# Blocks beyond the third of an expert: from every turn to the end of the stage

## The chip, the cores and the metric

The kernel runs on one core of a Trainium2 chip. TensorE (PE) multiplies matrices; PEld is its loading of weights. VectorE (DVE), ScalarE (ACT) and GpSimd (POOL) do the element-wise work, and SyncE (SP) issues most DMA transfers. Each engine runs its own list of instructions in order and waits for others at semaphores. The metric is the time of one execution on the device in microseconds (us).

## The reference

Two layers run over 512 tokens of width 1024 (256 latent, 256 context). Each layer mixes the tokens (convolutions, gating, attention) and then sends every token to two of 16 experts; the router is shared. The change concerns the experts of the first layer alone.

```python
def moe_ffn(h, w_router, router_bias, w_gate, w_up, w_down):
    """Sigmoid router with bias-corrected, group-limited selection: best group, then top-2 experts in it."""
    s = jax.nn.sigmoid((h @ w_router).astype(F32))
    sel = s + router_bias.astype(F32)
    grp = sel.reshape(*sel.shape[:-1], N_EXPERT_GROUPS, EXPERTS_PER_GROUP)
    grp_score = jnp.sum(lax.top_k(grp, GROUP_SCORE_TOPK)[0], axis=-1)
    best = jnp.argmax(grp_score, axis=-1)
    in_group = (jnp.arange(N_EXPERTS) // EXPERTS_PER_GROUP) == best[..., None]
    _, idx = lax.top_k(jnp.where(in_group, sel, -jnp.inf), TOP_K)
    w = jnp.take_along_axis(s, idx, axis=-1)
    w = w / jnp.sum(w, axis=-1, keepdims=True)
    gates = jnp.sum(jax.nn.one_hot(idx, N_EXPERTS, dtype=F32) * w[..., None], axis=-2).astype(h.dtype)
    y = jnp.zeros_like(h)
    for e in range(N_EXPERTS):
        a = jax.nn.silu(h @ w_gate[e]) * (h @ w_up[e])
        y = y + gates[..., e:e + 1] * (a @ w_down[e])
    return y
...
        hf = rms_norm(x_mid, norm2_g[l]) * (1.0 + sc2) + sh2
        x = x_mid + g2 * moe_ffn(hf, w_router, router_bias, exp_w_gate[l], exp_w_up[l], exp_w_down[l])

        if not last:
            spectra_ctx = hyena_filter_spectra(n_ctx, *filt)
            ctx_mid = ctx + cg1 * mix_tokens(proj_ctx, k_ctx, v_ctx, None, spectra_ctx, lp)
            hc = rms_norm(ctx_mid, norm2_g[l]) * (1.0 + csc2) + csh2
            ctx = ctx_mid + cg2 * moe_ffn(hc, w_router, router_bias, exp_w_gate[l], exp_w_up[l], exp_w_down[l])
```

## The kernel before

The expert stage of the first layer takes the experts one after the other, in the order of the table TURNS, each in one call of `turn_0` (L1671). An expert's tokens are done in blocks of 64 (BLK); P is 128. Since only the chip knows how many tokens an expert got, the counts `cnt` are computed there (L1373 and L1374) and each engine loads the count of the next turn into a register (`counted`, L1828) and branches on it:

- `tc.If(cv > BLK, label=f"turn{p}")` at L1736: with over 64 tokens the If is taken (two blocks), otherwise the Else (one block). The other side of the code is jumped over.
- inside the If, `tc.If(cv > P, ...)` at L1762 (L1754 in the last turn): a third block, with its own Else.
- inside that, `tc.If(cv > P + BLK)` at L1772 (L1757 in the last turn): `overflow` (L1612), a loop over all further blocks (L1640). Its code stands in each of the 16 turns.

`tc.mark_branch_hint_location` (L1729 for the turn's If, L1737 for the third block) puts a hint ahead of a branch, on PE, DVE and ACT. PE, DVE and ACT run in the order in which the code is written (`tc.manual_schedule`).

An expert's weights are six pieces of 1 MB, loaded on SP's queue by the class `Stream` (`main`). `done(n)` releases the n oldest pieces, and `pump` issues as many further loads as slots are free (L183), each waiting for the last use of its slot. Where the branch decides which code runs, `repeat` issues the same loads on the other sides (L202). So the loads of a turn follow its `main.done(4)` in SP's list: behind the third block where that is run, behind `main.repeat()` in each Else.

`mm_in` makes an expert's hidden values (its matmuls carry L1538), `mm_out` its outputs (L1562), `put` sends a block's outputs to memory (copy L1444, indirect DMA L1445), `turn` transposes gathered tokens (L1522). At the end of the last turn `parts` forms `st` from the last outputs (L1580, L1581) and `add` puts them to the token stream (matmuls L1591, adds L1596 and L1597), with `stat` on ScalarE (L1834). L574 makes a small table for the second layer. In the second layer the experts go through another function, with a branch at L1862 around its rarer blocks.

Of the kernel before, what the change touches and what calls it, by code (L numbers as in the profile page):

```python
# [22 lines left out]
NE = 16  # L23
# [100 lines left out]
def hybrid_block_kernel(ctx: ExitStack, tc: tile.TileContext, xin, const, fconst, par, fpar, misc, fng,  # L124
# [979 lines left out]
    def project(l, T, S, yh, yl, split, mm3, hx, hf, hp, spare):  # L1104
# [3 lines left out]
        with ExitStack() as pctx:  # L1108
# [261 lines left out]
            b2 = bank()  # L1370
            for t in range(T):
                nc.tensor.matmul(b2[:, :16], lhsT=ones, rhs=M[:, t], start=(t == 0), stop=(t == T - 1))
            cnt = rp.tile([P, 16], I32, name="cnt", tag="cnt")  # L1373
            V.tensor_copy(cnt, b2[:, :16])  # L1374
            if dump is not None:
                dump(f"sc{l}", sc.rearrange("p t e -> p (t e)"))
                dump(f"gw{l}", gw.rearrange("p t e -> p (t e)"))
# [12 lines left out]
    def moe(l, cnt, idx, gc, pd, pk, rk, hx, h0, hp):  # L1390
# [5 lines left out]
        with ExitStack() as mctx:  # L1396
# [274 lines left out]
            def turn_0(p, e, cv, w, b0):  # L1671
# [64 lines left out]
                with tc.If(cv > BLK, label=f"turn{p}") as branch:  # L1736
# [14 lines left out]
                    if last:  # L1751
                        parts(b1, more[0])
                        mm_out(w, AT[0], out)
                        with tc.If(cv > P, label=f"third{p}"):  # L1754
                            add(more, last=True)
                            block(e, w, turn(X, 0, BLK, h=h0), g3[:, e:e + 1], C("slot", 2, 3), *temp, last=True)
                            with tc.If(cv > P + BLK):  # L1757
                                overflow(e, w, cv, P + BLK, *temp, last=True)
                            zero(OT[1])
                        main.done(4)  # L1760
                    else:
                        with tc.If(cv > P, label=f"third{p}") as branch2:  # L1762
                            turn(X, 0, BLK, h=h0)
                            put(b1, rows[1][:, e:e + 1])
                            b3 = mm_in(w, h0, tag="tp")
                            act(b3, g3[:, e:e + 1], AM[1])
                            head(0)
                            spin(AM[1], AT[1])
                            head(1)
                            put(mm_out(w, AT[1], bank("ob")), rows3[:, e:e + 1])  # L1770
                            mm_out(w, AT[0], out)
                            with tc.If(cv > P + BLK):  # L1772
                                overflow(e, w, cv, P + BLK, *temp)
                            main.done(4)
                        with branch2.Else():
                            main.repeat()
                            put(b1, rows[1][:, e:e + 1])
                            head(0, 1)
                            mm_out(w, AT[0], out)
                with branch.Else():  # L1780
                    first({4: lambda: vector(0), 6: lambda: vector(1)})
                    main.repeat()
                    if last:
                        where(e, OT[0], C("slot", 0, 1))
                        where(e, OT[1], C("slot", 1, 2))
                    scaled()
                    if start:
                        spin(AM[0], AT[0])
                        mm_out(w, AT[0], out)
                        for q in (1, 2):  # L1790
                            prepare(q, 0)
                            prepare(q, 1)
                        head(0, 1)
                    else:
                        head(0)
                        prepare(p + 2, 0)
                        spin(AM[0], AT[0])
                        prepare(p + 2, 1)
                        head(1)
                        mm_out(w, AT[0], out)  # L1800
# [11 lines left out]
                if not last:  # L1812
                    main.done(2)
                    return ncv, nw, b2
                parts(out, ST[0])
                for t in range(T):
                    add(owed, more, only=[t], last=True)
                    if t:
# [317 lines left out]
```

## Time and profile before

| | us |
|---|---|
| median of three executions (1350.97 to 1355.32) | 1351.72 |
| the profiled execution: time | 1359.33 |
| the profiled execution: span | 1357.5 |
| PE busy in the span (85%) | 1156.3 |
| DVE busy | 537.9 |
| ACT busy | 314.8 |
| POOL busy | 294.3 |

The expert stage of the first layer lies between about 479 and 829 us of the span, the second layer behind it. The turns differ: turn 2 has a third block, turns 3, 10, 14 and 15 have two blocks, the other eleven have one. A view of waits names the instruction that stood still, what it was released by, and how long it stood; "issue" is waiting for nothing that the profile shows, and an engine's name with a q (PEq, DVEq, PEldq) is its queue of control instructions: branches (COMPARE_BRANCH), register loads (TENSOR_LOAD) and semaphores. Times of such instructions aren't in the busy times. The rows on which the prediction rests stand below.

### The profile page before, as it was taken

Reading aid. Unit: us, or ns where it says so; the run is one execution under the profiler, and the core shown is the slowest. Engines: PE = TensorE matmul, PEld = TensorE weight load, DVE = VectorE, ACT = ScalarE, POOL = GpSimd, SP = SyncE. Lnnn points to the kernel's source line nnn. Section 1 sums busy time; section 2 is a strip of 40 time slices with the busy share of each in tenths; the row PEclk is TensorE's granted clock in tenths of the full one; section 3 lists DMA queues with packets and bytes.
Section 4 is the critical chain, followed back from the end, with each engine's and each line's share of the span. In section 5 each row is a group of like instructions: output and inputs, shape, how many; then the busy total and the mean of one; then the engine's idle time right before and its main releaser. Section 6 shows DMA issues by size and latency. Waiting matters only on the chain. (4 is left out here: it accounts for less than half of the span.)

```text
span 1357.5 us, 16560 instructions
## 1 busy us (share of the span) xinstructions
PE 1156.3 (85%) x6205; PEld 646.1 (48%) x6205; DVE 537.9 (40%) x1068; ACT 314.8 (23%) x569; POOL 294.3 (22%) x238
## 2 busy tenths in 40 slices
PE   6799998888899788978898977878787799988985
PEld 2456565556688433323333424756675433332321
DVE  4430966335323521100011047685535244433444
ACT  2422233223212111001111115324423111111111
POOL 4332232322033121111112064434224000000000
PEclk9999998888799788988899996889868899998997
DMA  9574453312572786599999645211236399947961
GB/s 361 199 302 184 156 186 101 132 62 94 217 279 72 297 340 218 175 384 393 383 396 395 260 141 192 93 63 55 98 126 264 141 409 402 393 187 291 403 267 47
DMA packets 48574, 310.85 MB, mean 229 GB/s; under 512 B 6017, under 2 KB 6209, under 8 KB 14096
## 3 DMA queue, kind: packets, MB, share of 16 engines
q1 hardware_dynamic: 41936, 292.77, 55.7%
q0 software_dynamic: 6320, 15.27, 4.3%
q8 instruction: 105, 1.72, 0.5%
q10 hardware_dynamic: 144, 0.52, 0.1%
q14 instruction: 69, 0.57, 0.1%
HBM read 297.99 MB, written 12.32 MB: 229 GB/s over the span
## 5 line engine op out<-in xcount | busy, mean ns | idle before, releaser
L603 POOL TENSOR_TENSOR ws<-w,ws 128x1024 fp32r<-128x1024 f32 x50 | 121.4, 2440 | 218.0 <-ACT ws L602 200.7
L1538 PE MATMUL b_pj<-w,HE 128*64 128x512 f32 x416 | 109.7, 665 | 23.3 <-issue 23.3
L234 PE MATMUL b_pj<-hh,ws 128*128 128x512 f32 (+1 forms) x448 | 123.0, 364 | 1.1 <-POOL ws L603 1.1
L1562 PE MATMUL b_sc<-w,rows 128*64 128x512 f32 x448 | 106.2, 615 | 2.7 <-ACT rows L1552 2.7
L693 DVE SCALAR_TENSOR_TENSOR cacc<-gl,pr,cacc 128x512 f32<-128x512 f32 (+1 forms) x120 | 92.6, 772 | 2.6
L234 PEld LDWEIGHTS b_pj<-hh,ws 128*128 128x128 f32 x448 | 79.9, 199 | 21.0 <-issue 9.7
L234 PE MATMUL b_pj<-hl,ws 128*128 128x512 f32 (+1 forms) x224 | 78.8, 352 | 0.0
L1538 PEld LDWEIGHTS b_pj<-w,HE 128*64 128x64 f32 x416 | 34.5, 151 | 85.3 <-issue 83.9
L602 ACT ACTIVATE ws<-w 128x1024 fp32r<-128x1024 f32 x50 | 52.5, 1052 | 70.2 <-PE b_pj L234 44.6
L1600 DVE TENSOR_TENSOR x<-b_ob,x 128x512 f32<-128x512 f32 x68 | 44.0, 687 | 61.8 <-PE b_ob L1591 61.6
L277 POOL TENSOR_TENSOR rf<-rf,half 128x1 f32<-128x1 f32 x2 | 1.1, 552 | 309.1 <-DVE rf L276 309.1
L1538 PE MATMUL b_pj<-w,hf 128*64 128x512 f32 x224 | 56.6, 644 | 10.4 <-PEq L1862 7.6
L1562 PEld LDWEIGHTS b_sc<-w,rows 128*64 128x64 f32 x448 | 31.5, 141 | 62.0 <-issue 57.5
L1445 POOL DMA_INDIRECT sums<-y,rws x19 | 29.8, 1567 | 137.4 <-DVE y L1444 123.1
L1538 PE MATMUL b_pj<-w,x 128*64 128x512 f32 x224 | 55.6, 617 | 1.8 <-PEq L1862 1.0
L234 PE MATMUL b_md<-w,sT 128*32 128x256 f32 x704 | 54.2, 433 | 1.3 <-DVE mT L313 1.3
L1545 DVE SCALAR_TENSOR_TENSOR X<-X,gc,b_pj 64x512 f32<-64x512 f32 x16 | 12.1, 754 | 108.2 <-ACT X L1544 108.2
L1444 DVE COPY y<-b_sc 128x512 f32<-128x512 f32 x15 | 10.4, 692 | 102.9 <-PE b_sc L1562 62.3
L234 PEld LDWEIGHTS b_pj<-hl,ws 128*128 128x128 f32 x224 | 44.6, 199 | 5.3
L1591 PE MATMUL b_ob<-st,ohT 128*128 128x512 f32 x76 | 32.7, 496 | 16.3 <-DVE st L1581 9.3
L1544 ACT ACTIVATE X<-b_pj 64x512 f32<-64x512 f32 x16 | 9.4, 589 | 158.4 <-PE b_pj L1538 150.7
L1544 ACT ACTIVATE cst<-b_pj 64x512 f32<-64x512 f32 x17 | 10.1, 592 | 145.6 <-PE b_pj L1538 145.6
(471 smaller groups left out, 2070.4 us busy)
## 6 DMA issues: line engine op xcount, KB each, us to landing
w<-in_exps_dram SPq DMA_DIRECT2D x168, 1024.0 KB, 11.4
w<-in_ada_dram SPq DMA_DIRECT2D x48, 1024.0 KB, 4.8
w<-in_win_dram SPq DMA_DIRECT2D x16, 1024.0 KB, 5.1
hold<-in_exps_dram SPq DMA_DIRECT2D x12, 1024.0 KB, 15.8
w<-in_wout_dram SPq DMA_DIRECT2D x8, 1024.0 KB, 4.7
hf<-in_exps_dram SPq DMA_DIRECT2D x6, 1024.0 KB, 8.0
cst<-in_exps_dram SPq DMA_DIRECT2D x6, 1024.0 KB, 8.7
pr<-in_par_dram SPq DMA_DIRECT2D x2, 1461.5 KB, 8.9
```

Of the source, the lines that this page charges most:

```text
L234: nc.tensor.matmul(out_, lhsT=lhsT, rhs=rhs, **kw)
L602: nc.scalar.activation(wh[:, :n], src, AF.Copy)
L603: nc.gpsimd.tensor_tensor(wl[:, :n], src, wh[:, :n].bitcast(F32), op=OP.subtract)
L693: nc.vector.scalar_tensor_tensor(ac, gl[:, :, j:j + L], R("cvw", i * 31 + j, i * 31 + j + 1), ac, op0=OP.mult, op1=OP.add)
L1444: V.tensor_copy(y, b)
L1445: nc.gpsimd.indirect_dma_start(out=sums[:, :], out_offset=bass.IndirectOffsetOnAxis(ap=row, axis=0), in_=y, in_offset=None, bounds_check=1 ...
L1538: nc.tensor.matmul(b[64 * j:64 * j + 64], lhsT=x, rhs=w[k // 2][:, at:at + 512], start=(k == 0), stop=(k == 7), tile_position=(0, 64 * j))
L1544: nc.scalar.activation(a[64:], b[:64], AF.Silu)
L1545: V.scalar_tensor_tensor(a[64:], a[64:], gate[64:], b[64:], op0=OP.mult, op1=OP.mult)
L1562: nc.tensor.matmul(b[64 * j:64 * j + 64], lhsT=aT[:, f, :], rhs=w[4 + f // 2][:, at:at + 512], start=(f == 0), stop=(f == 3), tile_positio ...
L1591: nc.tensor.matmul(b, lhsT=ohT[:, t * P:(t + 1) * P], rhs=st[h], start=(i == 0), stop=(i == len(blocks) - 1))
L1600: V.tensor_tensor(y[:, cs], b, y[:, cs], op=OP.add)
```

## The change

The overflow test leaves the third block of every turn. The code runs once, after `parts` in the last turn, under one test of the largest count: `cnt` gets a 17th column with the maximum (a reduction and a copy on DVE, in both layers). Under that test there is, for each of the 16 experts, an If that loads the expert's six pieces of weights again and runs `overflow`. `main.done(4)` of the last turn moves behind it, out of the If of two blocks, and `main.repeat()` of the last turn's Else goes. Line numbers of the new kernel are three higher than the old from L1376 on, so that L1736 is its L1739, and L1581 its L1584; from the new test on they differ by more (the new test is at L1815, the 16 Ifs at L1820).

```diff
@@ -1370,8 +1370,11 @@
             b2 = bank()
             for t in range(T):
                 nc.tensor.matmul(b2[:, :16], lhsT=ones, rhs=M[:, t], start=(t == 0), stop=(t == T - 1))
-            cnt = rp.tile([P, 16], I32, name="cnt", tag="cnt")
-            V.tensor_copy(cnt, b2[:, :16])
+            cnt = rp.tile([P, 17], I32, name="cnt", tag="cnt")
+            V.tensor_copy(cnt[:, :16], b2[:, :16])
+            most = rt("most")
+            V.tensor_reduce(most[:, 0:1], b2[:, :16], axis=AX.X, op=OP.max)
+            V.tensor_copy(cnt[:, 16:17], most[:, 0:1])
             if dump is not None:
                 dump(f"sc{l}", sc.rearrange("p t e -> p (t e)"))
                 dump(f"gw{l}", gw.rearrange("p t e -> p (t e)"))
@@ -1754,10 +1757,7 @@
                         with tc.If(cv > P, label=f"third{p}"):
                             add(more, last=True)
                             block(e, w, turn(X, 0, BLK, h=h0), g3[:, e:e + 1], C("slot", 2, 3), *temp, last=True)
-                            with tc.If(cv > P + BLK):
-                                overflow(e, w, cv, P + BLK, *temp, last=True)
                             zero(OT[1])
-                        main.done(4)
                     else:
                         with tc.If(cv > P, label=f"third{p}") as branch2:
                             turn(X, 0, BLK, h=h0)
@@ -1769,8 +1769,6 @@
                             head(1)
                             put(mm_out(w, AT[1], bank("ob")), rows3[:, e:e + 1])
                             mm_out(w, AT[0], out)
-                            with tc.If(cv > P + BLK):
-                                overflow(e, w, cv, P + BLK, *temp)
                             main.done(4)
                         with branch2.Else():
                             main.repeat()
@@ -1779,7 +1777,8 @@
                             mm_out(w, AT[0], out)
                 with branch.Else():
                     first({4: lambda: vector(0), 6: lambda: vector(1)})
-                    main.repeat()
+                    if not last:
+                        main.repeat()
                     if last:
                         where(e, OT[0], C("slot", 0, 1))
                         where(e, OT[1], C("slot", 1, 2))
@@ -1813,6 +1812,17 @@
                     main.done(2)
                     return ncv, nw, b2
                 parts(out, ST[0])
+                with tc.If(nc.values_load(cnt[0:1, 16:17], engines=engs, min_val=0, max_val=N) > P + BLK):
+
+                    add(more, last=True)
+                    for q in range(NE):
+                        ce = counted(q)
+                        with tc.If(ce > P + BLK):
+                            for i in range(6):
+                                nc.sync.dma_start(w[i], source("exp", l, 6 * q + i))
+                            overflow(q, w, ce, P + BLK, *temp, last=True)
+                    zero(OT[1])
+                main.done(4)
                 for t in range(T):
                     add(owed, more, only=[t], last=True)
                     if t:
```

The list of SP in turn 2, before: the test at L1772 with the loop of `overflow` (L1640) stands between the branch of the third block and the loads of L183, and the two groups of L202 are those of the Else sides.

```order
L1736 COMPARE_AND_BRANCH
L1762 COMPARE_AND_BRANCH
L1772 COMPARE_AND_BRANCH
L1640 COMPARE_AND_BRANCH
L1640 UNCONDITIONAL_BRANCH x2
L2132 BRANCH_PREFETCH_HINT
L1640 REGISTER_ALU
L1640 COMPARE_AND_BRANCH
L1640 UNCONDITIONAL_BRANCH
L1772 UNCONDITIONAL_BRANCH
L183 DMA w<-in_exps_dram 128x2048 x2
L183 DMA hold<-in_exps_dram 128x2048 x2
```

What SP meets between the third block's branch and the next loads is, there, the test and its loop, each with waits for the other engines.

The same place after: the branch of the third block (now printed at L1762, as `branch2` starts three lines earlier) is followed by the loads.

```order
L183 DMA w<-in_exps_dram 128x2048
L1739 COMPARE_AND_BRANCH
L1762 COMPARE_AND_BRANCH
L183 DMA w<-in_exps_dram 128x2048 x2
L183 DMA hold<-in_exps_dram 128x2048 x2
L1762 UNCONDITIONAL_BRANCH
```

On SP, PE, DVE, ACT and POOL alike the test and the loop are gone from the place between the third block's last work and the release of the weights.

The list of DVE at the end of the last turn, before: the end of the If (L1736), the small table L574, `st` of L1581, and the first adds.

```order
L1718 TENSOR_TENSOR cst<-cst,G_3410 128x1024
L1736 UNCONDITIONAL_BRANCH
L574 SCALAR_TENSOR_TENSOR aT<-mT_69,msc 128x4 x4
L1581 TENSOR_TENSOR st_9314<-b_sc,st_9314 64x512
L1581 TENSOR_TENSOR st_9315<-b_sc,st_9315 64x512
L1596 TENSOR_TENSOR HE_3413<-b_ob,G_3410 128x512
```

After, the part ahead of the new test (HE, G and x are tiles; `st_7727` and `st_7728` are the halves of st):

```order
L1721 TENSOR_TENSOR cst<-cst,G_3413 128x1024
L1739 UNCONDITIONAL_BRANCH
L1584 TENSOR_TENSOR st_7727<-b_sc,st_7727 64x512
L1584 TENSOR_TENSOR st_7728<-b_sc,st_7728 64x512
L1815 TENSOR_LOAD cnt
L1815 COMPARE_AND_BRANCH
L1599 TENSOR_TENSOR HE_3416<-b_ob,G_3413 128x512
```

`st` has moved up, and the branch stands where L574 stood. The part behind the jump over the overflow block:

```order
L1820 UNCONDITIONAL_BRANCH
L1834 TENSOR_SCALAR ohT_3422<-cst 128x512
L1815 UNCONDITIONAL_BRANCH x2
L574 SCALAR_TENSOR_TENSOR aT<-mT_69,msc 128x4 x4
L1599 TENSOR_TENSOR HE_3416<-b_ob,G_3413 128x512
```

So `st` moves ahead of L574; the load of the largest count and the branch L1815 stand between them, and L574 stands between the branch and the first adds. The branch passes 571 rows of DVE's list. In the compiled program the jump of PE over the If of a turn passes 584 or 585 instructions before and 402 to 406 after in the turns that end in the Else (368 in turn 0), and the new jump at the end passes 3251.

## Rows read from the trace of the kernel before

**Rows 1.** Windows, core 0: stretch, its length, busy us (xcount) by engine, PEclk, DMA share, GB/s

```profile
540.00:560.00 20.00, 18.64 (x94) 6.50 (x92) 2.14 (x3) 2.17 (x4) 3.13 (x2) 1.00 0.14 17
...
580.00:620.00 40.00, 31.45 (x142) 11.52 (x140) 3.58 (x5) 4.34 (x8) 7.67 (x6) 0.91 1.03 381
620.00:660.00 40.00, 31.53 (x132) 11.28 (x130) 3.58 (x5) 4.33 (x8) 6.77 (x5) 0.89 1.02 394
```

**Rows 2.** Waits of PE from 484 to 800: who waited for whom, us, times, longest

```profile
PE b_pj L1538 <- issue: 25.8, 10, 5.8
...
PE b_pj L1538 <- DMA w<-in_exps_dram: 2.4, 1, 2.4
...
PE b_md L1538 <- DVE y L1444: 1.7, 1, 1.7
```

**Rows 3.** Branches of line L1736, all and from 485: count, ns min/median/max, first and last start

```profile
L1736 PEldq COMPARE_BRANCH  x16: 76/5946/7167, 488.4 to 782.0; - x16
...
L1736 PEldq COMPARE_BRANCH  x1: 3342/3342/3342, 488.4 to 488.4; - x1
```

**Rows 4.** Timeline of PE at 583 and 646: start, us, engine, line, operation [idle before]

```profile
582.32 2.74 PE L1562 MATMUL b_sc<-w,rows 128*64 128x512 f32 x12
590.89 1.97 PE L1538 MATMUL b_pj<-w,HE 128*64 128x512 f32 x4 [5.83 <-issue]
...
645.88 2.36 PE L1538 MATMUL b_pj<-w,HE 128*64 128x512 f32 x10 [0.91 <-issue]
```

**Rows 5.** Other branches of PE, lines L1772, L1762 and L1754, columns as in rows 3

```profile
L1772 PEldq COMPARE_BRANCH  x1: 243/243/243, 555.5 to 555.5; - x1
...
L1762 PEldq COMPARE_BRANCH  x8: 68/376/2271, 538.7 to 781.4; - x8
...
L1754 PEldq COMPARE_BRANCH  x2: 187/1816/3444, 804.3 to 808.9; - x2
```

**Rows 6.** Page, part 3: the instruction queue: packets, MB, share

```profile
q8 instruction: 105, 1.72, 0.5%
```

**Rows 7.** Waits of the DMA queue of SyncE from 470 to 830

```profile
SPq L183 <- PEq L1772: 35.6, 1, 35.6
```

**Rows 8.** Line L1538 from 484 to 800: the projections that use h, columns as in rows 3

```profile
L1538 PE MATMUL b_tp<-w,h x16: 592/592/643, 543.0 to 546.1; 128*64 128x512 f32 x16
...
L1538 PE MATMUL b_tp<-hold,h x16: 592/592/593, 546.5 to 549.5; 128*64 128x512 f32 x16
```

**Rows 9.** Timeline of VectorE (DVE) at 560

```profile
560.09 0.69 DVE L1444 COPY y<-b_sc 128x512 f32<-128x512 f32 x1 [2.83 <-PEq L1772]
```

**Rows 10.** Timelines of PE, DVE and GpSimd (POOL) at 805 to 817, and line L574

```profile
805.10 3.60 PE L1562 MATMUL b_sc<-hold,rows 128*64 128x512 f32 x16
815.50 0.80 PE L1591 MATMUL b_ob<-st,ohT 128*128 128x512 f32 x1 [6.80 <-DVE st L1581]
...
810.99 3.75 DVE L574 SCALAR_TENSOR_TENSOR aT<-mT,msc 128x4 f32<-128x4 f32 x4 [0.74 <-DVEq L1754]
...
816.11 0.69 DVE L1581 TENSOR_TENSOR st<-b_sc,st 64x512 fp32r<-64x512 f32 x1 [0.66 <-ACT st L1580]
816.83 0.69 DVE L1596 TENSOR_TENSOR HE<-b_ob,G 128x512 f32<-128x512 f32 x1
...
814.60 1.99 POOL L1719 TENSOR_TENSOR x<-x,cst 128x1024 f32<-128x1024 f32 x1
...
L574 DVE SCALAR_TENSOR_TENSOR aT<-mT,msc x4: 148/764/2301, 811.0 to 814.6; 128x4 f32<-128x4 f32 x4
```

**Rows 11.** DVE: the cast of the counts, and the loads of a count into a register

```profile
479.19 0.17 DVE L1374 CAST cnt<-b_tp 128x16 int32<-128x16 f32 x1 [1.59 <-PE b_tp L1372]
...
L1828 DVEq TENSOR_LOAD <-cnt x16: 300/306/582, 482.0 to 760.1; - x16
```

**Rows 12.** Branches of line L1862 (second layer), and who waited for them (us, times)

```profile
L1862 PEldq COMPARE_BRANCH  x16: 89/3386/6276, 1062.4 to 1340.7; - x16
...
  PE b_pj L1538: 17.6, 12
```

## Prediction

> **What bounds the kernel now.** I read the busy times by stage first. In the expert stage of the first layer TensorE (PE) works 31.45 and 31.53 us of two 40 us stretches while the DMA engines are full, and 18.64 of 20 where they are nearly idle [rows 1]. So something takes PE's time there, and the view of waits says what: the matmuls of L1538 stood still 25.8 us in ten places "on issue", that is on nothing but PE's own queue, and once 2.4 us on a weight load [rows 2]. The branch instruction of L1736 explains these: PE's 16 take from 76 ns to 7.17 us, median 5.95 [rows 3]. The cheap ones are in the five turns that go into the If (more than 64 tokens), the dear ones in the eleven that jump over it to the Else. The timeline shows one at its worst: matmuls end at 585.06, the next starts at 590.89, 5.83 us later, and nothing else was late [rows 4]. Usually the branch begins while matmuls of some 3.6 us are still queued, so that of 6 us about 2.4 are seen. Weights land in time all along; a faster load gives nothing by itself. VectorE, ScalarE and GpSimd matter at the two ends of the stage alone.
>
> **What the change takes out of the turns.** In the compiled program PE's jump over the If passes 584 instructions in the old kernel and about 404 in the new one, because some 180 instructions of overflow code leave every turn. What does a jump of 404 cost? The rows give both ends. A jump of 179 (L1772) took 0.24 us, those of L1762 (up to 354, announced long ahead by a hint) 0.38 us in the median [rows 5]. The jump of 584 takes 3.34 us with idle DMA engines and 6 to 7 with busy ones [rows 3]. Instructions arrive in packets of 16.4 KB (1.72 MB in 105) [rows 6], which is 256 instructions of 64 bytes. A jump of 584 (2.28 packets) always lands two or three packets on; one of 404 (1.58) lands in the very next packet when it starts in the first 42% of its own, and two on otherwise. A next packet comes in order anyhow during a turn of 15 us, so I count such a jump as one of the cheap rows, and the others as they are now. The ten turns with a gap lose 25.8 + 2.4 - 0.9 (one wait of 0.91 us that lies inside a turn [rows 4]) = 27.3 us, 2.7 us each, 2.4 without the worst. With 42% of ten I take four turns at 2.4: **-9.7 us**, with bounds 0 (every turn still fetches) and -27.3 (none does).
>
> [...]
>
> **Turn 2, the only one with a third block.** There the old kernel tests for overflow (L1772) and finds none; nothing of the overflow code ran in the trace. SyncE waited 35.6 us at that test for PE before it issued four weight loads [rows 7]; the slots' last matmuls had started at 546.1 and 549.5 [rows 8], and PE was through with the test just before 560.09, where VectorE's copy goes on [rows 9]. The loads go 10 to 15 us earlier in the new kernel, into a stretch where the DMA share was 0.14 [rows 1]. That fills slack and makes later branches meet fewer transfers, for which I count nothing apart from the bound above. That copy of L1444 had waited 2.83 us for PE [rows 9], and PE then waited 1.7 us for the copy [rows 2]. Without the test the copy follows its matmuls: **-1.7 us**, bounds -2.83 and 0.
>
> **What is added at the end of the stage.** All five engines now load the largest count and jump over the whole overflow block (L1815 of the new kernel). The load takes 0.31 us [rows 11]. On VectorE four small operations of L574 and all adds of L1596 stand behind that branch; on GpSimd the adds of L1597; on ScalarE the squares; on SyncE three loads of the second layer's experts, whose first branch comes at 1062 [rows 12], 240 us of cover. PE ran out of matmuls at 808.7 and waited until 815.50 for st of L1581 [rows 10], so its own far jump of 3.4 us (the row at 804.3 [rows 5]) is hidden. VectorE did L574 from 810.99 to 814.74, then st, and the first L1596 at 816.83. L574's four operations on 128x4 numbers take 148 ns at the least and 2.30 us at the most, beside GpSimd's large additions; the last of them starts at 814.6, with GpSimd's last addition [rows 10]. I read that as waiting for GpSimd. Now st comes first, done at about 813.0 (two operations of 0.69 and 0.66 us between); with the load the jump starts at 813.3. The trace shows no such jump on VectorE (571 rows of the program). If it takes 0.06 us, as VectorE's short ones, L574 again waits for GpSimd, whose last addition ends at 816.59, and L1596 starts where it did. At 3.4 us, as PE with idle DMA engines, L574 is quick by then and L1596 starts at 817.3. At 6.1 us it starts at 820.0. I take 3.4, since the DMA engines are quiet there: **+0.5 us**, bounds 0 and +3.2.
>
> **The wider count tile.** A reduction and a copy follow the cast of 0.17 us at 479.19 on VectorE [rows 11], in both layers, and PE and SyncE wait for that tile: 0.4 us each time, **+0.8 us**, bounds 0 and +1.2.
>
> **The second layer** is not edited but moves in the program, by about 350 PE instructions. Its branches (L1862) cost between 89 ns and 6.28 us, and PE waited 17.6 us after them in twelve places [rows 12]. Which of them are dear depends on where they fall; I count 0, bounds -5 and +8.
>
> **Sum.** -9.7 - 1.7 + 0.5 + 0.8 = -10.1 us. The profiled run took 1359.33 us for a span of 1357.5, 7.6 us over the median of 1351.72, and would become 1349.2; from the median, 1341.6 us.
>
> **The rivals.** *Every jump over the If still fetches.* [...] Against it: no jump that lands in the next packet costs more than 2.27 us in the rows. Then only -1.7 + 0.5 + 0.8 = -0.4 remains: 1351.3 us. [...] Chance 0.27.
>
> *No jump over the If shows any more*, since a fetch that meets quieter DMA engines (3.3 to 3.6 us) hides behind the 3.6 us of queued matmuls. For it: the four loads that come earlier. Against it: weights of 6 MB a turn keep the DMA share at 1.02 [rows 1], and will again after two or three turns. -27.3 - 0.4 = -27.7: 1324 us. Chance 0.08.
>
> *Slower, by the second layer's branches.* Some 14 jumps are taken there and show 17.6 us. Were each to show the 2.4 us of the first layer, they would show 33.6, 16 more; half of that, 8 us, with none of the first layer's jumps saved, gives 1351.3 + 8 = 1359 us. It decides the sign from two to three more dear branches on if nothing is saved before, from six or seven if four turns are. For it: the jumps there keep their 584 instructions. Against it: a shift can as well free those that are dear now. Chance 0.12.
>
> *The overflow code runs* (an expert over 192 tokens) can't be on these inputs: the third-block test was passed by turn 2 alone, whose overflow test went by in 0.24 us.
>
> **How the numbers follow.** About 0.3%, 4 us, is what a measurement of this kernel can tell from no change. The forecast (two to seven turns saved) has 0.53 and lies between 1335 and 1347.5; with the second rival, faster has 0.61. Same has the first rival's 0.27, slower 0.12. For eight in ten the range runs from 1331, which leaves out the rival without stalls, to 1356, which leaves out the slower one.
>
> **What would show it.** Right: PE's branches of the turn's If fall below 0.5 us in about four of eleven turns and stay near 6 in the rest; the waits "on issue" of the first projection shrink from 25.8 to about 16; no gap at 560; the four loads issued by about 550; the first add after the stage no more than 1 us later. Wrong: eleven branches near 6 us as before, or VectorE held over 4 us at the new branch, or longer waits behind the branches of the second layer.

## The result and the profile after

The change made the kernel slower. Fifteen runs of each gave medians of 1365.21 us (after) and 1357.42 us (before), a ratio of 1.0055 with a 95% interval of 1.0032 to 1.0077, some 7.5 us. The three runs known before the prediction had a median of 1351.72, at the low end of the 1350.97 to 1361.76 that before showed in the end. The prediction was 1341.6 us, its range 1331 to 1356.

The profiled execution of after has a span of 1366.1 us. To find where the time went I cut the trace of each kernel at five marks: PE's first branch of a turn's If, the end of the last output matmul of the last turn, the second layer's first matmul (L238), its first branch around the rarer blocks, and the end. The last column is PE's idle time in front of the projections (L1538, after the change L1541) of the second layer's turns, added up from the trace's instructions; most of it is directly behind the branches. The rows of the view of waits add up to 0.1 to 1.4 us more (18.9 for before, 30.8 for after). The rows "again" are second profiles of the same kernels.

| us | turns | end of stage | mixing of layer 2 | experts of layer 2 | idle behind its branches |
|---|---|---|---|---|---|
| before | 320.3 | 20.5 | 233.2 | 295.1 | 18.1 |
| before, again | 320.4 | 20.5 | 233.1 | 302.6 | 22.6 |
| after | 313.4 | 26.3 | 232.7 | 306.7 | 29.7 |
| after, again | 312.7 | 26.3 | 231.4 | 310.5 | 30.5 |

By the means of two profiles each, the turns gained 7.3 us, the end of the stage lost 5.8, the mixing gained 1.1, and the experts of the second layer, which nobody edited, lost 9.8: together +7.2 us, near the 7.5 us of the ratio. The stretch ahead of the first mark is not in the table: it took 488.4 and 483.9 us before, 487.0 and 482.8 after, so that the spans of these four profiles differ by 5.9 us.

**The turns.** The branches of the turn's If in after: all, those of turns 0 and 1, and the three of turns 11 to 13 (columns as in rows 3, which they answer).

```profile
L1739 PEldq COMPARE_BRANCH  x16: 76/3635/7989, 487.0 to 773.0; - x16
...
L1739 PEldq COMPARE_BRANCH  x2: 376/466/556, 487.0 to 499.8; - x2
...
L1739 PEldq COMPARE_BRANCH  x3: 2895/4375/5183, 705.0 to 733.9; - x3
```

Turns 0 and 1 now take 0.56 and 0.38 us, where before none of the eleven took less than 3.3. Turns 11 to 13 take 5.18, 4.38 and 2.89 instead of 6. The other six stay between 5.5 and 8 us. In the view of waits of PE in the stage, this answers rows 2:

```profile
PE b_pj L1541 <- issue: 23.8, 8, 7.8
PE b_ob L1525 <- DMA G<-hbuf,idx: 5.8, 1, 5.8
...
PE b_tp L1554 <- DVEq L1739: 1.7, 1, 1.7
```

The waits "on issue" went from ten places to eight and, with the one on a weight load, from 28.2 to 23.8 us. A wait for gathered tokens (G) grew from 3.4 us to 5.8, and the one of 1.7 us in turn 0, for VectorE's branch, stayed. PE's busy time over the stretch went from 280.6 and 279.6 us (before and its second profile) to 276.8 and 277.3, so that of the 7.3 us some 3 lie in the matmuls themselves and the rest in waits.

**Turn 2.** SyncE's list (issue of weights) and PE's around the old place of the overflow test:

```profile
520.76 25.03 SPq L183 DMA_DIRECT2D w<-in_exps_dram  x4
547.18 2.04 SPq L183 DMA_DIRECT2D hold<-in_exps_dram  x2
```

```profile
555.06 3.60 PE L1565 MATMUL b_sc<-w,rows 128*64 128x512 f32 x16
558.50 4.03 PE L1541 MATMUL b_md<-w,HE 128*64 128x512 f32 x18
```

The held loads were issued by 549, against 561 to 562, and PE goes from L1565 (before: L1562) to the next projection without idle time. The wait of 1.7 us in rows 2 is gone.

**The end of the stage.** VectorE's and PE's timelines, which answer rows 10:

```profile
806.44 0.69 DVE L1584 TENSOR_TENSOR st<-b_sc,st 64x512 fp32r<-64x512 f32 x1 [0.66 <-ACT st L1583]
813.74 0.38 DVE L574 SCALAR_TENSOR_TENSOR aT<-mT,msc 128x4 f32<-128x4 f32 x4 [6.62 <-SPq L1815]
814.16 0.69 DVE L1599 TENSOR_TENSOR HE<-b_ob,G 128x512 f32<-128x512 f32 x1
```

```profile
796.77 3.60 PE L1565 MATMUL b_sc<-hold,rows 128*64 128x512 f32 x16
810.23 0.77 PE L1594 MATMUL b_ob<-st,ohT 128*128 128x512 f32 x1 [9.87 <-DVEq L1815]
```

VectorE was done with st at 807.1 and then stood 6.62 us, for SyncE. PE's last matmul ended at 800.4; its first matmul of `add` started 9.87 us later, released by VectorE's jump. What L1815 itself did on each engine:

```profile
L1815 SPq EVENT_SEMAPHORE  x7: 17/17/17, 813.1 to 813.6; - x7
L1815 POOLq EVENT_SEMAPHORE  x6: 17/30/43, 813.0 to 813.4; - x6
...
L1815 DVEq EVENT_SEMAPHORE  x2: 21/21/21, 810.1 to 810.2; - x2
...
L1815 PEldq COMPARE_BRANCH  x1: 3476/3476/3476, 801.2 to 801.2; - x1
...
L1815 DVEq COMPARE_BRANCH  x1: 56/56/56, 806.8 to 806.8; - x1
...
L1815 SPq COMPARE_BRANCH  x1: 53/53/53, 807.2 to 807.2; - x1
L1815 POOLq COMPARE_BRANCH  x1: 45/45/45, 807.4 to 807.4; - x1
...
  DVE aT L574: 6.6, 1
```

SyncE met the branch at 807.2, and its next instruction on that line ran at 813.1: 5.9 us for a jump over the overflow block. GpSimd needed 5.6 us (807.4 to 813.0), VectorE 3.3 (806.8 to 810.1), PE 3.48. SyncE had issued a load of constants of 1.5 MB just before (L531 at 806.8), and the DMA share was 0.74 from 808 to 810 and 1.04 from 810 to 812, against 0.04 from 801 to 806, while PE jumped. In the trace L574 stands behind waits for eight semaphores, and SyncE's instructions from 813.1 on move six of them, the last at 813.60; L574 starts at 813.74. I read them as the counters that the skipped loads of weights would have moved. So VectorE waited for SyncE's jump though it needs no data from it.

**The count tile.** The two new operations end 0.27 us after the cast:

```profile
477.91 0.17 DVE L1374 CAST cnt<-b_tp 128x16 int32<-128x16 f32 x1 [1.59 <-PE b_tp L1372]
478.00 0.17 DVE L1376 TENSOR_REDUCE most<-b_tp 128x1 f32<-128x16 f32 x1
478.20 0.15 DVE L1377 CAST cnt<-most 128x1 int32<-128x1 f32 x1
```

**The second layer.** PE's waits there, for after and, below it, for its second profile and that of before (first profile: 13.0 on PEq L1862 and 4.5 on ACTq L1862, together the 17.6 of rows 12 to rounding):

```profile
PE b_pj L1541 <- PEq L1872: 23.1, 13, 5.9
...
PE b_pj L1541 <- PEq L1879: 3.9, 1, 3.9
...
PE b_pj L1541 <- issue: 3.5, 1, 3.5
```

```profile
PE b_pj L1541 <- PEq L1872: 23.5, 13, 5.8
...
PE b_pj L1541 <- issue: 3.4, 1, 3.4
PE b_pj L1541 <- PEq L1879: 3.3, 1, 3.3
```

```profile
PE b_pj L1538 <- PEq L1862: 20.8, 12, 6.2
```

The line L1872 of after is L1862 of before, L1879 its branch around a third block. The sum of 23.1 + 3.9 us stands against 18.1 and 21.3 us of before (17.6 and 20.8, and 0.5 at its third block, L1869). The 3.5 us on "issue" lie inside turn 4 and begin 2.7 us behind the end of its branch; before has no such wait in a projection.

### The profile page after: what moved, and what is told of

It is laid out like the page before. It is cut to its first block, busy times and chain, and to the rows that moved or that the text cites. A ratio compares the mean times of both kernels' runs of the same rounds, so it can differ in the third digit from the quotient of the medians.

```text
span 1366.1 us, 16566 instructions
## 1 busy us (share of the span) xinstructions
PE 1152.2 (84%) x6205; PEld 643.8 (47%) x6205; DVE 538.9 (39%) x1072; ACT 314.6 (23%) x569; POOL 295.4 (22%) x238
## 5 line engine op out<-in xcount | busy, mean ns | idle before, releaser
L1541 PE MATMUL b_pj<-w,HE 128*64 128x512 f32 x416 | 107.6, 658 | 22.0 <-issue 22.0
L1565 PE MATMUL b_sc<-w,rows 128*64 128x512 f32 x448 | 106.0, 614 | 2.7 <-ACT rows L1555 2.7
L1541 PEld LDWEIGHTS b_pj<-w,HE 128*64 128x64 f32 x416 | 33.6, 149 | 81.6 <-issue 80.3
L1541 PE MATMUL b_pj<-w,hf 128*64 128x512 f32 x224 | 57.0, 648 | 17.3 <-PEq L1872 13.4
L1541 PE MATMUL b_pj<-w,x 128*64 128x512 f32 x224 | 57.3, 626 | 7.5 <-PEq L1872 4.0
L1565 PEld LDWEIGHTS b_sc<-w,rows 128*64 128x64 f32 x448 | 31.5, 140 | 61.8 <-issue 57.3
```

What stands on the lines that cost most here:

```text
L1541: nc.tensor.matmul(b[64 * j:64 * j + 64], lhsT=x, rhs=w[k // 2][:, at:at + 512], start=(k == 0), stop=(k == 7), tile_position=(0, 64 * j))
L1565: nc.tensor.matmul(b[64 * j:64 * j + 64], lhsT=aT[:, f, :], rhs=w[4 + f // 2][:, at:at + 512], start=(f == 0), stop=(f == 3), tile_positio ...
```

## The experiments

Two theories stood at the start. **Far jump**: what the end of the stage lost is SyncE's jump over the block, for which VectorE waits. **Position**: what the second layer lost comes from where its PE code lies relative to the packets of 16.4 KB [rows 6] in which PE's instructions arrive. Of these packets (queue q8) 20 start between 45.68 and 454.24 us in the trace of before, where PE takes no branch; from the first to the last PE ran 4853 instructions in 19 steps, 255 a packet (2407 matmuls, 2406 weight loads, 40 semaphores; 4852 in after), near the 256 that I count with. By my count of the compiled program, which no trace shows, the second layer's first branch lies at 74.75 packets before and at 76.12 after, 0.375 of a packet further on, apart from whole packets. The rival of the second was that the waits follow the transfers of the single execution. The third question was which part of the change gave the turns their 7 us.

| us | turns | end of stage | experts of layer 2 | idle behind its branches | ratio to before (95%) |
|---|---|---|---|---|---|
| after | 313.4 | 26.3 | 306.7 | 29.7 | 1.0055 (1.0032 to 1.0077) |
| after_hint | 313.9 | 22.4 | 310.5 | 28.2 | 1.0052 (1.0021 to 1.0082) |
| after_nofinal | 310.9 | 20.9 | 303.1 | 26.2 | 0.9996 (0.9968 to 1.0025) |
| before_pad | 317.9 | 20.5 | 306.3 | 29.6 | 1.0052 (1.0020 to 1.0083) |
| after_pad | 309.5 | 27.2 | 289.6 | 17.3 | 0.9947 (0.9912 to 0.9981) |
| after_dead | 320.2 | 28.9 | 288.5 | 16.9 | 1.0047 (1.0011 to 1.0083) |
| hint_pad40 | 307.5 | 22.3 | 299.0 | 22.2 | 0.9962 (0.9927 to 0.9997) |
| hint_pad32 | 310.7 | 22.4 | 299.0 | 23.8 | 0.9983 (0.9946 to 1.0020) |
| hint_pad48 | 310.7 | 22.3 | 302.6 | 24.8 | 0.9994 (0.9960 to 1.0028) |
| hint_sp | 307.5 | 25.9 | 306.1 | 27.9 | one run |
| hint_rest | 313.1 | 28.1 | 308.8 | 28.5 | one run |

**The far jump: a hint ahead of it.**

```diff
@@ head of the last turn
+                if last:
+                    top = nc.values_load(cnt[0:1, 16:17], engines=engs, min_val=0, max_val=N)
+                    tc.mark_branch_hint_location("over", top > P + BLK, engines=[ET.SP, ET.Pool, ET.DVE, ET.Activation])
@@ end of the last turn
-                with tc.If(nc.values_load(cnt[0:1, 16:17], engines=engs, min_val=0, max_val=N) > P + BLK):
+                with tc.If(top > P + BLK, label="over"):
```

> The changed kernel with the largest count loaded at the head of the last turn and a branch hint for the test at the end put there, on SyncE, GpSimd, VectorE and ScalarE. Theory of the far jump (SyncE needs 5.9 us to jump over the overflow block, from 807.2 to 813.1, and VectorE's L574 waits for SyncE until 813.7): the jump of SyncE falls under 1 us, L574 starts at once behind VectorE's own jump, and the stretch from PE's last matmul of the stage to VectorE's first add shrinks from 13.8 us to about 9 to 10; the kernel becomes 4 to 5 us faster than the changed one, about 1360 us against 1357 of before. Rival (SyncE is held by its load of constants or by transfers, not by the jump): the stretch stays near 13.8 us.

Instructions of SyncE, GpSimd and VectorE on the test (L1818 there), and VectorE's timeline:

```profile
L1818 SPq EVENT_SEMAPHORE  x7: 17/17/17, 808.6 to 809.1; - x7
L1818 POOLq EVENT_SEMAPHORE  x6: 17/30/43, 808.6 to 809.0; - x6
...
L1818 DVEq EVENT_SEMAPHORE  x2: 21/21/21, 808.4 to 808.6; - x2
...
L1818 DVEq COMPARE_BRANCH  x1: 71/71/71, 805.5 to 805.5; - x1
L1818 POOLq COMPARE_BRANCH  x1: 68/68/68, 808.1 to 808.1; - x1
L1818 SPq COMPARE_BRANCH  x1: 68/68/68, 808.2 to 808.2; - x1
```

```profile
809.24 0.38 DVE L574 SCALAR_TENSOR_TENSOR aT<-mT,msc 128x4 f32<-128x4 f32 x4 [3.10 <-SPq L1818]
809.84 0.69 DVE L1599 TENSOR_TENSOR HE<-b_ob,G 128x512 f32<-128x512 f32 x1 [0.22 <-PE b_ob L1594]
```

SyncE and GpSimd pass in 0.5 us, counted from PE's last matmul L574 starts 4.2 us earlier than in after, and the end of the stage falls from 26.3 to 22.4 us, as the theory said (9.8 us to the first add instead of 13.8). VectorE's own jump hardly changed, 2.9 us with the hint against 3.3. The total did not follow: 1.0052, when some 1.0025 was to be expected. The second layer's experts took 310.5 us in that profile, as long as in any, and the interval takes in both values.

**The far jump: no test at all.**

```diff
@@ end of the last turn
                 parts(out, ST[0])
-                with tc.If(nc.values_load(cnt[0:1, 16:17], engines=engs, min_val=0, max_val=N) > P + BLK):
...
-                    zero(OT[1])
                 main.done(4)
```

> The changed kernel without the test and the overflow block at the end (blocks beyond the third of an expert are left out altogether; these inputs have none). Theory of the far jump: the stretch from PE's last matmul of the stage to VectorE's first add falls from 13.8 us to 8 or less, as before the change (8.1) or better. The turns keep what they gained (7 us from the first branch to the last matmul). Since the block of 3251 PE instructions is gone, the second layer's code falls on other positions: by the theory of positions its waits behind the branches change (before 17.6, after 27 us); by the rival (they are set by transfers at the time) they stay near 27. Total between 1345 and 1358 us.

PE's timeline at the end of the stage:

```profile
789.81 3.60 PE L1565 MATMUL b_sc<-hold,rows 128*64 128x512 f32 x16
800.73 0.80 PE L1594 MATMUL b_ob<-st,ohT 128*128 128x512 f32 x1 [7.32 <-DVE st L1584]
```

From the end of the last matmul (793.4) to the first add it is 7.32 us, against 9.87 in after; the first add of VectorE comes 8.6 us after it, where 8 or less was expected, and the whole end takes 20.9 us against 20.5 before. So the test at the end costs 5.4 to 5.8 us, and 4 of them are jumps that a hint spares. The second layer is on a third position (63.41 packets) with 26.2 us, which doesn't decide between the theory and its rival. The kernel without the test is level with before, not faster, though it gained 9.4 us in the turns.

**Whose jump.** The same edit as after_hint with the hint for SyncE alone, and for the other three alone.

> The changed kernel with the largest count loaded at the head of the last turn and the hint there for SyncE alone. Theory (SyncE's jump over the overflow block is what holds VectorE's L574): SyncE passes in under 1 us, and the stretch from PE's last matmul to VectorE's first add is near 10 us, as with the hint on four engines (9.8), and not 13.8. VectorE's own jump of some 3 us stays and is seen instead. Rival (GpSimd's jump of 5.6 us, or its semaphore of 1.27 us, matters too): 12 to 14 us.

> The same with the hint for GpSimd, VectorE and ScalarE, and none for SyncE. Theory: SyncE needs 5.9 us for its jump again and the stretch stays at 13 to 14 us, although the other three are through in under 3 us. Rival: about 10 us.

VectorE's timeline with the hint for SyncE alone:

```profile
805.40 0.38 DVE L574 SCALAR_TENSOR_TENSOR aT<-mT,msc 128x4 f32<-128x4 f32 x4 [2.94 <-DVEq L1818]
806.17 0.69 DVE L1599 TENSOR_TENSOR HE<-b_ob,G 128x512 f32<-128x512 f32 x1 [0.39 <-PE b_ob L1594]
...
808.99 0.69 DVE L1599 TENSOR_TENSOR h<-b_ob,G 128x512 f32<-128x512 f32 x1 [1.40 <-POOLq L1818]
```

and with the hint for the other three, with SyncE's instructions below it:

```profile
815.36 0.38 DVE L574 SCALAR_TENSOR_TENSOR aT<-mT,msc 128x4 f32<-128x4 f32 x4 [9.11 <-SPq L1818]
815.77 0.69 DVE L1599 TENSOR_TENSOR HE<-b_ob,G 128x512 f32<-128x512 f32 x1
```

```profile
L1818 SPq EVENT_SEMAPHORE  x7: 17/17/17, 814.7 to 815.2; - x7
...
L1818 SPq COMPARE_BRANCH  x1: 53/53/53, 808.3 to 808.3; - x1
```

Without a hint for SyncE, its jump takes 6.4 us and L574 waits 9.11 us for it, although the rest is through; the first add comes 15.6 us behind PE's last matmul, later than expected. With it, L574 waits 2.94 us for VectorE's own jump, and the first add comes at 10.7 us. That shows SyncE as the engine that mattered first. The rival keeps a part: two adds later VectorE waits 1.40 us for GpSimd's unhinted jump, and the whole end takes 25.9 us, hardly less than 26.3. The 4 us came only where SyncE and GpSimd both had the hint. VectorE's and ScalarE's jumps took 2.9 and 2.6 us with it (after_hint) and 3.0 and 2.4 without (hint_sp), so their hints bought nothing that shows; hints for SyncE and GpSimd alone were not run.

**Position: dead code alone.** In before, 88 small matmuls (352 PE instructions) that never run:

```diff
@@ last turn, before
                             with tc.If(cv > P + BLK):
+                                pb = bank()
+                                for _ in range(88):
+                                    nc.tensor.matmul(pb[:16, :16], lhsT=ident[:, :16], rhs=ident[:, :16], start=True, stop=True)
                                 overflow(e, w, cv, P + BLK, *temp, last=True)
```

> The kernel before with 88 small matmuls (352 PE instructions) put into the overflow code of the last turn, which never runs, so that the second layer's PE code lies where it lies in the changed kernel, to within three instructions. Nothing else is changed. Theory of positions: PE's waits behind the second layer's branches rise from 17.6 to about 27 us and the kernel becomes 7 to 10 us slower (ratio 1.005 to 1.008). Rival (the waits follow transfers and timing of the single execution): the waits stay at 17 to 20 us and the ratio within 0.998 to 1.003.

PE's waits in the second layer:

```profile
PE b_pj L1538 <- PEq L1865: 24.0, 14, 5.8
...
PE b_pj L1538 <- PEq L1872: 3.4, 1, 3.4
```

24.0 + 3.4 us against 18.1 and 21.3 in the two profiles of the kernel before, and a ratio of 1.0052: code that is never run made the kernel as slow as the change did. Now the other way round, 40 small matmuls (160 instructions) in after, in the block that never runs:

```diff
@@ end of the last turn, after
                 with tc.If(nc.values_load(cnt[0:1, 16:17], engines=engs, min_val=0, max_val=N) > P + BLK):
 
+                    pb = bank()
+                    for _ in range(40):
+                        nc.tensor.matmul(pb[:16, :16], lhsT=ident[:, :16], rhs=ident[:, :16], start=True, stop=True)
                     add(more, last=True)
```

> The changed kernel with 40 small matmuls (160 PE instructions) put into the overflow block at the end, which never runs, so that the second layer's PE code lies two packets of 256 instructions behind its place in the kernel before, that is on the same position within a packet. Theory of positions: the waits behind the second layer's branches fall from 27 to about 18 us, and the kernel becomes 8 to 9 us faster than the changed one, about equal to before (ratio 0.998 to 1.002). Rival: they stay near 27 us and the ratio near 1.0055.

```profile
PE b_pj L1541 <- PEq L1875: 11.9, 10, 4.1
...
PE b_pj L1541 <- ACT st L1583: 4.9, 3, 1.6
```

11.9 + 4.9 us, and 17.3 behind all branches. With the second layer back on its old position the change is a gain: 0.9947, better than predicted for this run. The 17 us between before_pad and after_pad in the experts' time (306.3 and 289.6) are more than the 12 between their idle times behind branches. All idle time of PE in that stretch is 51.9 and 39.1 us, 12.8 apart; the other 3.9 lie in the matmuls, 254.4 and 250.5 us for the same number. TensorE's granted clock stood at the lower of its two levels (0.5 of full speed; the traces of before and after have 0.5 and 1.0 alone) for 42 us of the stretch in before_pad and for 32 in after_pad, so the kernel with the longer stalls also multiplied at the lower clock for longer.

**Does it repeat?**

> The kernel before once more, for a second profile: how far the price of each branch of the second layer repeats. Theory of positions: the same branches are dear as in the first profile, and the sum behind them is 18.1 us to within 3. Rival (timing of the single execution): another pattern, and a sum between 17 and 30.

> The changed kernel once more, for a second profile. Theory of positions: the same branches dear as in its first profile, a sum behind them of 28 to 31 us (29.7 then, 28.2 in the variant with the hint, which lies on the same position). Rival: another pattern, and a sum between 17 and 30. The end of the stage keeps its 13.8 us to within 1.

After repeats: 29.7 and 30.5 us, with the dear branches (over 4.5 us) in the same turns but one: turns 1, 2, 6, 7 and 11 in both, turn 12 in the second alone. Before repeats less well: 18.1 and 22.6, with turn 1 at 2.2 us in one profile and 6.3 in the other, the rest alike. So the profile that I predicted from was the cheaper of the two. Their experts' times differ by 7.5 us (295.1 and 302.6), half of it idle time (43.2 and 47.0), half of it matmul time (251.9 and 255.7). All profiles together, by position: 16.9 to 22.6 us on the old one (five profiles), 27.9 to 30.5 on that of after (six), and in between on the two next to the old one. But which branches are dear does not follow from the position: before_pad lies where after lies, to within three instructions by my count, and its dear ones are those of turns 1, 5, 6, 11 and 12; on the old position they are those of turns 3, 9, 10 and 14 in before and of 3, 4, 5 and 14 in after_pad and after_dead. The old position with both repairs, and its two neighbours:

> The changed kernel with the hint at the head of the last turn and the 160 dead PE instructions that put the second layer on its old position within a packet. Theory: both repairs add up, 9.8 us from the last matmul to the first add instead of 13.8, about 17 us behind the second layer's branches instead of 28 to 30: ratio to before 0.990 to 0.993, some 1345 us. Rival (the gain of the position alone was luck of one build): 0.998 to 1.005.

> As hint_pad40, with 128 dead PE instructions instead of 160: the second layer lies 0.125 of a packet before its old position. By the theory of positions the waits behind its branches take some value of their own between 17 and 30 us, nearer to 17 as its neighbour in position, and the total follows them one to one from hint_pad40. Rival (only timing): as hint_pad40 or as the changed kernel, at random.

> As hint_pad40, with 192 dead PE instructions: the second layer lies 0.125 of a packet behind its old position. By the theory of positions the waits behind its branches again differ and the total follows them one to one; a value between those of hint_pad40 (17 us) and of the changed kernel (28 to 30, which lies 0.375 behind) is expected, about 20. Rival (only timing): no such order.

These three are after_hint with 40, 32 and 48 of the dead matmuls of after_pad. PE's waits with 40:

```profile
PE b_pj L1541 <- PEq L1878: 19.7, 11, 6.1
```

22.2, 23.8 and 24.8 us, where 17, some more than 17, and 20 were expected. The steps are smaller than the 4.5 us between two profiles of before, so the order shows nothing. hint_pad40 is faster than before (0.9962), but not by the sum of both repairs (0.990 to 0.993 was expected); the branch of turn 1 was dear in it, and its ratio and that of after_pad can't be told apart. That code which never runs moves the time of code behind it is shown by the totals of before_pad and after_pad, and the idle time goes with the position between about 20 and 29 us. That the position within a packet is what makes a branch dear is not shown; that, and the 5 us between profiles on one position, stay open.

**What gave the turns their 7 us.** After with a test in each turn behind the release of the weights, whose 45 small matmuls never run; and 58 of them in the block at the end, so that the second layer lies where it did before.

```diff
@@ third block of each turn but the last, after
                             main.done(4)
+                            with tc.If(cv > P + BLK):
+                                pb = bank()
+                                for _ in range(45):
+                                    nc.tensor.matmul(pb[:16, :16], lhsT=ident[:, :16], rhs=ident[:, :16], start=True, stop=True)
```

> The changed kernel, but each turn gets a test with 45 small matmuls (180 PE instructions) that never run, behind the release of the weights: the jump over the If is 584 to 588 instructions long again, as before the change, while the loads stay early. 58 more at the end put the second layer on the position it has in the kernel before. Theory (the 7 us that the turns gained come from the shorter jump and the fetches it spares): from the first branch to the last matmul of the stage it takes 318 to 321 us again, against 313.4 changed and 320.3 before, with PE branches near 3.5 and 6 us in all eleven turns. Rival (they come from the four weight loads that are issued earlier, and from the test that no longer holds SyncE): the stretch stays at 312 to 315 us. The end of the stage keeps its 13.8 us, the second layer has about 18 us behind its branches, as before; total 1.002 to 1.006 by the theory, about 0.997 by the rival.

PE's branches of the turn's If, and its waits in the stage:

```profile
L1739 PEldq COMPARE_BRANCH  x16: 76/5767/8492, 488.1 to 781.9; - x16
```

```profile
PE b_pj L1541 <- issue: 30.1, 10, 8.2
...
PE b_md L1541 <- DVE y L1447: 1.7, 1, 1.7
```

The turns take 320.2 us, as before, with ten waits of 30.1 us. The wait of 1.7 us at turn 2 is back, too, since the new test brings it. The four loads are still early (held pieces issued by 550). One profile can carry this only because its spread can be accounted for. The ten profiles with the short jump have 307.5 to 313.9 us for the turns, the four with the long one 317.9 to 320.4, and within each group the shorter ones are those in which the granted clock stood less long at its lower level: about 38 us in before, after_dead and after alike (320.3, 320.2 and 313.4), 27 to 34 us in the kernels below 311. So the gain came from the length of the jump, with turn 2's test a part of it, and the earlier loads gave nothing that shows. The end of the stage did not keep its 13.8 us in this run: the first add came 16.4 us behind PE's last matmul, with a jump of SyncE of 7.2 us; so of the total of 1.0047, which is where the theory put it, 2.6 us are a longer end (28.9 instead of 26.3).

## Why the prediction was wrong

**What bounds the kernel** was read rightly: PE's branches. In the turns and in the second layer the large terms are such jumps (27.3 and 18.1 us of PE's idle time in before, 23.8 and 29.7 in after); at the end of the stage it is the jumps of SyncE, GpSimd and VectorE (5.9, 5.6 and 3.3 us in after).

**The turns: the mechanism right, the size too large.** Four turns of the ten were to become cheap, 9.7 us (four times 2.4 is 9.6; nothing hangs on it). By my count of positions, which no trace shows, the jumps that land in the next packet are those of turns 0, 1, 11, 12 and 13, and these did become shorter; in turn 0 PE still waits for VectorE's branch. The others stayed near 6. But only turns 0 and 1 fell to the price of the cheap rows; in turns 11 to 13 the branch still took 2.9 to 5.2 us. In the DMA records of after no packet of q8 starts while the branches of turns 0 and 1 run. In turns 11 to 13 one starts 2.8, 1.9 and 0.5 us after the branch began (3.5, 3.5 and 3.6 in before), against 3.4 to 3.7 in turns 6 to 9, and in all of them the branch ends 1.3 to 1.6 us after the packet is there. I read that as the next packet asked for earlier and still not there. The step "a next packet comes in order anyhow during a turn of 15 us, so I count such a jump as one of the cheap rows" is what failed. A packet does come without a branch: in turns 5 to 8 of before one starts 5.8 to 5.9 us behind the one at the branch, with no branch there. But in turns 11 to 13 of after the packet was there 1.4 us after the branch began at the earliest, too late for it. Whether that hangs on how near the branch stands to the start of its packet, no run shows. Idle time in front of the ten turns went from 27.3 to 23.8 us, -3.5 instead of -9.7, with turn 4 worse by 2.0 and turn 11 by 1.4. The rest of the stretch's -6.9 us in these two profiles is turn 2 (-1.7), a wait of 0.9 us inside a turn that went, 2.4 us more for gathered tokens, and some 3.4 us less matmul time, which I had not counted on and can't explain from these rows.

**Turn 2**: -1.7 us, right, and the loads moved as said, and gave nothing by themselves, as said.

**The end of the stage: +0.5 predicted, bounds 0 and +3.2, measured +5.8.** VectorE's own jump took 3.3 us, what I had taken. L574 was quick once GpSimd's additions were over (0.38 us for four instead of 3.75), as I had read it. The step that failed is the list of who waits for whom: I put behind VectorE's branch only what stands behind it on VectorE and did not ask for which other engine's skip L574 waits. SyncE's jump of 5.9 us was priced at nothing, because its three loads have 240 us of cover, and so was GpSimd's of 5.6, which holds the end of the stage as long when SyncE's is spared (25.9 us instead of 26.3). The quiet DMA engines, on which the 3.4 us rested, weren't quiet from 808 us on (share 0.74, then 1.04 from 810 to 812).

**The count tile**: two operations, 0.27 us by the timeline instead of 0.4; too little to be seen in the total.

**The second layer: 0 predicted, bounds -5 and +8, measured +9.8.** This is the largest error. The rival that ends slower named it, with a price of 8 us and a chance of 0.12, and combined it with no saving in the first layer. The mechanism had a row (branches from 89 ns to 6.28 us, rows 12), and the term was put at nothing without a reason for either sign. The runs show in its place that moving the code is enough: 352 instructions that never run cost 1.0052. That the rival's +7.3 us comes near the measured +7.5 is luck, since it saves only turn 2's 1.7 us in the turns and loses half a microsecond at the end of the stage. The two profiles of before also show that 17.6 us was the low end of its own spread. With the measured terms the sum is -7 for the turns and turn 2, +6 for the end of the stage, +10 for the second layer and -1 for the mixing: +7 or +8, and not -10. Of the signs of being wrong two came, VectorE held for 6.62 us at the new branch and longer waits in the second layer; of those of being right, the gap at 560 that went and the loads issued by 550.

**The reference.** The three runs of before that I started from had a median of 1351.72; all fifteen have 1357.42. Of the 23.6 us between 1341.6 and 1365.2 this is 5.7; the other 18 are the terms above.

## What to carry to other kernels

Ask of a block that is only ever skipped what the jump over it costs on every engine, SyncE and GpSimd too, and what waits for that jump. Here the five engines took 2.7 to 5.9 us each for it (after), and VectorE's L574 stood 6.62 us for SyncE's. Where something waits, try a hint ahead of the test: here it took SyncE and GpSimd from 5.9 and 5.6 us to 0.5 and left VectorE and ScalarE at 2.9 and 2.6. Code taken out or put in moves what lies behind it, and in a loop that is bound by PE and branches in each turn that weighed more here than the edit: the turns gained 7.3 us and the second layer, not edited, lost 9.8, and code that never ran made before 0.5% slower and after 1.1% faster. So time an edit with some dead code at two or three positions before judging it. One profile of such a kernel gives one draw of these stalls, and of the clock (18.1 and 22.6 us behind the second layer's branches in two of before, 251.9 and 255.7 us of matmuls): take two before working out a sum of a few microseconds.

## What the runs showed of the hardware

- Jumps over one block of code took 3.48 us on PE while the DMA engines were nearly idle (share 0.04 from 801 to 806), 2.7 on ScalarE (806.2 to 808.9), 3.3 on VectorE, and 5.9 on SyncE and 5.6 on GpSimd, which jumped while the share rose to 0.74 and above. With a hint in the code of the turn's start they took 0.5 us on SyncE and GpSimd and still 2.9 on VectorE and 2.6 on ScalarE; why the hint spares only two of the four stays open.
- 352 instructions that never run made the kernel 0.5% slower, and 160 made the changed one 1.1% faster (0.9947 against 1.0055).
- Operations of 128x4 numbers on VectorE took 3.75 us for four beside GpSimd's additions [rows 10] and 0.38 us for four when GpSimd had no operation running (after, 813.74).
- PE's matmuls of the second layer's experts, the same number, took 250.5 us with 32 us of the stretch at the lower granted clock (after_pad) and 254.4 us with 42 us (before_pad).
